# Two SwiGLU layers of a hybrid decoder: sums, norm rows and weight sums at other places, and the SP and GpSimd queues in the order of the program

## The chip, the cores and the metric

The kernel runs on one core of a Trainium2 chip. The metric is the device time of one execution in microseconds (us); the median of three runs of the kernel before is 1213.38 us, from 1211.77 to 1215.27.

## The reference

A decoder trunk of two layers over 512 tokens of width 1024, in float32:

```
h = h + recurrent_mixer(rms_norm(h, a_norm))
h = h + swiglu(rms_norm(h, a_ffn_norm), a_ffn_w_in, a_ffn_w_out)
k, v = shared_kv(h, ...)
h = h + dilated_attention_mixer(rms_norm(h, b_norm), ..., k, v, cos, sin)
h = h + swiglu(rms_norm(h, b_ffn_norm), b_ffn_w_in, b_ffn_w_out)

def swiglu(h, w_in, w_out):
    g, u = jnp.split(h @ w_in, 2, axis=-1)
    return (jax.nn.silu(g) * u) @ w_out
```

The hidden width of both SwiGLU layers is 2816, that is 22 blocks of 128. cos and sin are tables made from the token positions; only the attention reads them.

## The kernel before

**Precision.** Every float32 matrix is split into a high and a low part (`xh`, `xl` of the activations, `wh`, `wl` of a weight), and each product is three matmuls (`mm3`, L185 to L187). A weight of 512 KB goes HBM -> `wr` by DMA, `wr` -> `wh` by ScalarE (CAST, L133), and `wl = wr - wh` by VectorE (L140). There are two `wr` buffers and three of `wh` and `wl`.

**One SwiGLU layer** (`swiglu`, used twice; FFN1 and FFN2 below) is a list of steps. Four *plain* steps come first: blocks 0, 22, 1 and 23 of `h @ w_in`, with weights `plain 0` to `plain 3` (24 matmuls each). Then come five rounds of seven products in the manner of Strassen and Winograd, each for four hidden blocks: the weights of the products are GA, GB (gate halves), UB (an up half), and sums of them: S1 and S3 are loaded as a sum (one plain load from SP, then an accumulating DMA from GpSimd on top, L655 and L657), S2 = S1 + GA and S4 = GB + S2 are made in place by VectorE (L667). The activations' side of these sums are T1 to T4, made from `h`. A step "O" multiplies a finished chunk by `w_out` and subtracts it from `h`; a step "L" splits a chunk that has come back turned. Round 0 is `GA GB O S1 S2 O S3 S4 UB`, rounds 1 to 3 are `S1 GA GB L S2 O O S3 O S4 O UB`.

**What the norm needs.** The sum of squares `ssum` goes through four matmuls (L318) and nine small VectorE instructions (`norm_factors`); then eight VectorE instructions write two diagonal tiles (`dgh`, `dgl`), and two matmuls with ones spread the factors over the partitions into `rb` (`norm_rows`, L332 to L340). In FFN1 and FFN2 these two matmuls stand behind the third plain block. `rb` scales the plain blocks (`plain_pair`).

**What sets the order.** Inside `swiglu` TensorE, VectorE and ScalarE run in the order in which the program is written (`manual_schedule`). SP and GpSimd, which issue the DMAs, are not in that set: the scheduler of the compiler orders their queues. All plain loads go through SP's queue; an instruction there that waits for a buffer holds up those behind it. The big tiles GA, GB, S1, S3 and UB have one buffer each, in memory that the layer ahead of the SwiGLU gives back with its last `ssum` addition (L310). `Stream.load_to(i)` loads all pieces up to number i, counted from the first weight of the kernel; `swiglu` first sets how far loads (`al`, 4 pieces) and splits (`asp`, 2) run ahead.

**Tables.** `rotary` makes the cos and sin tables with some 30 small VectorE instructions at the first finished block of FFN1's last stage.

Of the kernel before, what the change touches and what calls it, by code (L numbers as in the profile page):

```python
# [20 lines left out]
ALU = mybir.AluOpType  # L21
# [36 lines left out]


class Held:  # L60


    def __init__(self, tc, engine):
        self.tc, self.engine, self.mark = tc, engine, None

    def __getattr__(self, op):
        fn, mark = getattr(self.engine, op), self.mark

        def run(*a, **k):
            inst = fn(*a, **k)  # L70
            behind(self.tc, inst, mark)
            return inst
        return run if mark is not None else fn
# [99 lines left out]
def trunk(tc, A, out):  # L173
    nc = tc.nc
    V, S, G, PE = Held(tc, nc.vector), Held(tc, nc.scalar), nc.gpsimd, nc.tensor

    def hold(mark, *fns):
        V.mark = S.mark = mark
        for fn in fns:
            fn()  # L180
        V.mark = S.mark = None
# [61 lines left out]
    with tc.tile_pool(name="keep", bufs=1) as kp, tc.tile_pool(name="wts", bufs=3) as wp, \  # L243
# [82 lines left out]
        def norm_rows(pool, r, tag="sq", bufs=1, copy=S.copy, hold=None, low=None, keep=None):  # L326
            dh, dl = (pool.tile([128, T], F32R, name=n, tag=g, bufs=b)
                      for n, g, b in (("dgh", tag, bufs), ("dgl", *(low or ("dgl", 1)))))
            ps = bank("O")
            for n in range(4):  # L330
                c = slice(128 * n, 128 * n + 128)
                V.tensor_scalar(dh[:, c], ident, r[:, n:n + 1], None, ALU.mult)  # L332
                a = V.scalar_tensor_tensor(dl[:, c], ident, r[:, n:n + 1], dh[:, c].bitcast(F32),
                                           ALU.mult, ALU.subtract)
            if hold:
                ws.hold[hold] = a
            PE.matmul(ps, ones_r, dh, start=True, stop=False)
            PE.matmul(ps, ones_r, dl, start=False, stop=True)
            rb = (keep or pool).tile([128, T], F32, name="rb", bufs=1)
            copy(rb, ps)  # L340
            return rb

# [14 lines left out]
        with tc.tile_pool(name="lru", bufs=2) as lp, \  # L357
# [66 lines left out]
            first.append(in_block(3, between=lambda: soon(norm_rows, lp, norm[0], "q", 3, V.tensor_copy, 4, ("q", 3))))  # L424
# [158 lines left out]
        def swiglu(fp, p, after):  # L583
# [75 lines left out]
            def split_weights(q, name, kk, hi, lo):  # L659
                n = name[:2]  # L660
                home = {"S2": "S1", "S4": "GB"}.get(n, n)

                def half(n):
                    return raws[q, n][:, :, 256 * kk:256 * kk + 256]

                def add(n, other):
                    V.tensor_tensor(half(n), half(n), half(other), ALU.add)  # L667

                if q == 0 and n in ("S2", "S4"):
                    add(*{"S2": ("S1", "GA"), "S4": ("GB", "S1")}[n])  # L670
                r = half(home).rearrange("q b (k c) -> q k b c", k=2)
                hi, lo = (x.rearrange("q (k b c) -> q k b c", k=2, b=4) for x in (hi, lo))
                S.copy(hi, r)  # L673
# [11 lines left out]
            def plain_block(j, b, i):  # L685
# [30 lines left out]
            def results(q, half, up, part):  # L716
# [5 lines left out]
                for i in range(2):  # L722
                    j = 2 * half + i
                    p.mark = V.transpose(turned[q][:, :, j], part[:, i].rearrange("q (b i) -> q b i", i=32))
# [18 lines left out]
            def product(q, name, first):  # L743
# [13 lines left out]
                if n in ("GA", "S2", "S3"):  # L757
                    part = acc["after " + n, q] = pair_tile()
                    for i in range(2):
                        S.copy(part[:, i], ps[i])  # L760
                        if n == "S3":
                            V.tensor_tensor(part[:, i], acc["S1", q][i], part[:, i], ALU.add)  # L762
# [9 lines left out]
            def out_block(c, m, i):  # L772
# [4 lines left out]
                for b in range(nb):  # L777
                    ps = bank("mm")
# [8 lines left out]
            for n in ("GA", "GB", "S1", "S3", "UB"):  # L787
                fetch(0, n)
            early = {0: make_t1, 1: make_t23, 2: low_t23, 3: lambda: plain_pair(0), 4: lambda: plain_pair(1),
                     6: lambda: (make_t4(), halve(d0, *homes["T4"]))}  # L790
            ordered = {mybir.EngineType.PE, mybir.EngineType.DVE, mybir.EngineType.Activation}
            with tc.manual_schedule(engines=ordered):
                for s, (kind, *what) in enumerate(p.steps):
                    {"plain": plain_block, "product": product, "out": out_block, "parts": parts_of}[kind](*what)
                    early.get(s, lambda: None)()

# [12 lines left out]
        with tc.tile_pool(name="tables", bufs=1) as rp:  # L809
            rp = Pool(rp)  # L810
            with tc.tile_pool(name="ffn1", bufs=2) as fp:
                fp = Pool(fp)
                tables = []

                def after_f1(m, ps):
# [3 lines left out]
                    if m == 0:  # L819
                        tables.extend(rotary(tc, A, rp, Temps(fp), p_f1.mark))  # L820

                swiglu(fp, p_f1, after_f1)
# [21 lines left out]
N_TMP = 5  # L844
# [7 lines left out]
def rotary(tc, A, rp, tp, mark):  # L852

    nc = tc.nc
# [4 lines left out]
    behind(tc, S.dma_start(far, A["far"]), mark)  # L859
    grow = rp.tile([128, 6, 128], F32, name="grow", bufs=1)  # L860
    behind(tc, S.dma_start(grow, A["row_gains"]), mark)
    V.tensor_scalar(grow[:, 3:6], grow[:, 3:6], -(128.0 ** -0.5), None, ALU.mult)


    pos = rp.tile([128, 8], I32, name="pos", bufs=1)
    behind(tc, S.dma_start(pos, A["pos"]), mark)
    inv = rp.tile([128, 16], F32, name="inv", bufs=1)
    behind(tc, S.dma_start(inv, A["inv_freq"]), mark)
    posf = rp.tile([128, 8], F32, name="posf", bufs=1)
    V.tensor_copy(posf, pos)  # L870
# [3 lines left out]
    tmp = [tp.tile([128, 512], F32, name="rtmp", tag="e", bufs=N_TMP) for _ in range(2)]  # L874
    ang, a1, a0, s1, k2, t = (tmp[i % 2][:, 128 * (i // 2):128 * (i // 2) + 128] for i in range(6))
# [15 lines left out]
    fma(s1, a0, -(2.0 ** 14), ang)  # L891
    rounded(a1, a0, 2.0 ** -9)
    fma(a0, a1, -512.0, a0)
    fma(s1, a0, m0[0], s1)
    fma(s1, a1, m1[0], s1)
    rounded(k2, s1, 1.0 / two_pi)
    fma(s1, k2, -c3[0], s1)
    fma(s1, a0, m0[1], s1)
    fma(s1, a1, m1[1], s1)
    fma(s1, k2, -c3[1], s1)  # L900
    rounded(t, s1, 1.0 / two_pi)
    fma(s1, t, -c3[0], s1)
    fma(s1, t, -c3[1], s1)
    V.tensor_add(k2, k2, t)
    fma(s1, a0, m0[2], s1)
    fma(s1, a1, m1[2], s1)
    fma(s1, k2, -c3[2], s1)
    V.scalar_tensor_tensor(t, s1, -1.0, s1, ALU.mult, ALU.max)
    V.tensor_scalar(t, t, -0.5, math.pi / 2.0, ALU.mult, ALU.add)
    S.activation(s1, s1, AF.Sin, scale=0.5)  # L910
    S.activation(t, t, AF.Sin)
    V.tensor_mul(a0, s1, t)
    V.tensor_mul(a1, s1, s1)
    for c in range(2):
        V.tensor_scalar(ss[:, :, c, :], a0.rearrange("q (c f) -> q c f", f=16), 4.0 * c - 2.0, None, ALU.mult)
# [446 lines left out]
```

## Time and profile before

| | |
|---|---|
| median of three runs | 1213.38 us |
| the profiled execution: its time | 1215.45 us |
| its span, first to last instruction | 1213.6 us |
| TensorE busy | 1171.2 us, 97% |
| VectorE busy | 854.5 us, 70% |
| ScalarE busy | 622.2 us, 51% |
| granted TensorE clock, mean | 0.987 |

The profiled execution took 1.85 us more than its span. The rows below name an engine, a line of the kernel and an operation, written as out<-in: `wl<-wr,wh` writes `wl`. PE is TensorE, DVE VectorE, ACT ScalarE, POOL GpSimd; SPq is the queue of DMA issues on SP. A timeline row begins with its start and its length in us; in brackets stands how long the engine was idle before and what ended that. "DMA to landing" is the time from the issue of a transfer to the arrival of its last byte.

### The profile page before, as it was taken

What the parts mean: (1) busy time and instruction counts of PE and PEld (TensorE: products, weight loads), DVE (VectorE), ACT (ScalarE), POOL (GpSimd) and SP (SyncE); (2) the same over time, 40 slices, a digit from 0 to 9 for tenths busy, and PEclk for the clock granted to TensorE, in tenths of its full rate; (3) what the DMA queues carried; (4) which work ended last, traced back from release to release, by engine and by line L of the source; (5) the groups of instructions that cost most, each with busy time, mean ns of one, the idle gap of its engine ahead of it and who ended that gap; (6) DMA issues with size and microseconds to landing.
All of it is one profiled execution on the core that took longest, in us unless ns stands there. A gap on an engine that the chain in (4) does not pass through costs nothing.

```text
span 1213.6 us, 15155 instructions
## 1 busy us (share of the span) xinstructions
PE 1171.2 (97%) x5403; PEld 961.5 (79%) x5403; DVE 854.5 (70%) x1525; ACT 622.2 (51%) x901; POOL 188.3 (16%) x221
## 2 busy tenths in 40 slices
PE   9999988899999999999999999999888999999998
PEld 6788876778888887788888887898767788888877
DVE  7987666686868686987565677765766867676764
ACT  6796444353535353575555677655443535353532
POOL 4210010110101000020411334341101101010000
PEclk9999999899999999999999999999898999999999
DMA  6643391857575732432988657435818575757224
GB/s 234 149 105 105 111 270 36 223 159 192 155 191 156 192 85 72 119 116 87 214 185 180 140 119 171 104 71 135 263 36 224 170 192 155 193 151 197 73 59 133
DMA packets 92235, 179.62 MB, mean 148 GB/s; under 512 B 8704, under 2 KB 27008, under 8 KB 92160
## 3 DMA queue, kind: packets, MB, share of 16 engines
q1 hardware_dynamic: 72144, 130.23, 33.3%
q0 software_dynamic: 18864, 47.19, 22.1%
q10 hardware_dynamic: 1152, 1.23, 0.4%
q8 instruction: 43, 0.70, 0.2%
q14 instruction: 32, 0.26, 0.1%
HBM read 164.99 MB, written 2.10 MB: 138 GB/s over the span
## 4 chain that ended last, share of the span: by engine, by line
PE 82%; DVE 9%; ACT 4%; DMA 3%; issue 2%; POOL 0%; DVEq 0%; ACTq 0%; POOLq 0%
PE ps L187 22%; PE ps L186 22%; PE ps L185 22%; PE ps L1025 5%; PE ps L1026 5%; PE ps L1027 5%; DMA S<-in_f_in 2%; DVE wl L674 1%; ACT wh L673 1%; PE ps L1104 1%; PE ps L1191 1%; DVE wl L140 1%; DVE xc L468 1%; ACT wh L133 1%; ACT pr L1177 0%
## 5 line engine op out<-in xcount | busy, mean ns | idle before, releaser
L133 ACT CAST wh<-wr 128x1024 fp32r<-128x1024 f32 (+2 forms) x136 | 131.0, 969 | 128.6 <-PE ps L186 77.9
L185 PE MATMUL ps<-wh,xh 128*128 128x512 f32 x320 | 126.8, 396 | 7.5 <-DVE e L762 7.5
L186 PE MATMUL ps<-wl,xh 128*128 128x512 f32 x320 | 126.4, 395 | 0.0
L187 PE MATMUL ps<-wh,xl 128*128 128x512 f32 x320 | 126.3, 395 | 0.0
L185 PE MATMUL ps<-gh,wh 128*128 128x512 f32 x288 | 113.9, 396 | 3.3 <-DVE h L785 3.3
L187 PE MATMUL ps<-gh,wl 128*128 128x512 f32 x288 | 114.6, 398 | 0.3
L186 PE MATMUL ps<-gl,wh 128*128 128x512 f32 x288 | 113.7, 395 | 0.0
L140 DVE TENSOR_TENSOR wl<-wr,wh 128x1024 fp32r<-128x1024 f32 (+2 forms) x93 | 99.9, 1084 | 15.8 <-ACT wh L133 15.4
L657 POOL DMA_DIRECT2D S<-in_f_in x40 | 48.4, 1290 | 386.8 <-DMA S<-in_f_in 167.9
L674 DVE TENSOR_TENSOR wl<-S,wh 128x1024 fp32r<-128x1024 f32 x60 | 73.3, 1225 | 47.2 <-ACT wh L673 47.2
L185 PE MATMUL ps<-xh,wh 128*128 128x512 f32 x256 | 103.5, 406 | 1.0 <-ACT xh L296 1.0
L673 ACT CAST wh<-S 128x1024 fp32r<-128x1024 f32 x60 | 62.8, 1050 | 79.3 <-PE ps L186 21.9
L185 PE MATMUL ps<-wh,T 128*128 128x512 f32 x240 | 95.6, 398 | 7.0 <-ACT wh L673 7.0
L186 PE MATMUL ps<-xl,wh 128*128 128x512 f32 x256 | 102.2, 399 | 0.1
L187 PE MATMUL ps<-xh,wl 128*128 128x512 f32 x256 | 101.9, 398 | 0.0
L186 PE MATMUL ps<-wl,T 128*128 128x512 f32 x240 | 95.8, 399 | 2.1 <-DVE wl L674 2.0
L187 PE MATMUL ps<-wh,T 128*128 128x512 f32 x240 | 95.0, 396 | 0.0
L1025 PE MATMUL ps<-wh,xh 128*128 128x512 f32 x224 | 91.5, 408 | 0.0
L1027 PE MATMUL ps<-wh,xl 128*128 128x512 f32 x224 | 87.8, 392 | 0.0
L1026 PE MATMUL ps<-wl,xh 128*128 128x512 f32 x224 | 87.4, 390 | 0.0
L673 ACT CAST wh<-GB 128x1024 fp32r<-128x1024 f32 x40 | 42.1, 1054 | 76.1 <-PE ps L187 50.9
L783 DVE TENSOR_TENSOR h<-h,ps 128x512 f32<-128x512 f32 x64 | 43.5, 685 | 51.4 <-PE ps L187 51.4
(284 smaller groups left out, 2702.9 us busy)
## 6 DMA issues: line engine op xcount, KB each, us to landing
S<-in_f_in SPq DMA_DIRECT2D x40, 512.0 KB, 4.7
S<-in_f_in POOLq DMA_DIRECT2D x40, 512.0 KB, 8.1
wr<-in_f_out SPq DMA_DIRECT2D x36, 512.0 KB, 4.4
wr<-in_w_q SPq DMA_DIRECT2D x28, 512.0 KB, 6.8
wl<-in_w_q POOLq DMA_DIRECT2D x28, 512.0 KB, 7.5
GA<-in_f_in SPq DMA_DIRECT2D x20, 512.0 KB, 4.6
GB<-in_f_in SPq DMA_DIRECT2D x20, 512.0 KB, 5.8
UB<-in_f_in SPq DMA_DIRECT2D x20, 512.0 KB, 5.2
```

The lines of the kernel that those rows point to most:

```text
L133: nc.scalar.copy(hi[:, c], r[:, c])
L140: a = eng.tensor_tensor(lo[:, c], r[:, c], hi[:, c].bitcast(F32), ALU.subtract)
L185: PE.matmul(ps, wh, xh, start=first, stop=False, skip_group_check=on)
L186: PE.matmul(ps, wh, xl, start=False, stop=False, skip_group_check=on)
L187: PE.matmul(ps, wl, xh, start=False, stop=last, skip_group_check=on)
L657: nc.gpsimd.dma_start(c, p.part(1, q, n == "S1", i), accum_op=ALU.add)
L673: S.copy(hi, r)
L674: V.tensor_tensor(lo, r, hi.bitcast(F32), ALU.subtract)
L783: V.tensor_tensor(by_time(x), by_time(x), in_turn(ps), ALU.subtract)
L1025: PE.matmul(ps[t], xh[k][:, r], wh[:, c], start=k == 0, stop=False)
L1026: PE.matmul(ps[t], xh[k][:, r], wl[:, c], start=False, stop=False)
L1027: PE.matmul(ps[t], xl[k][:, r], wh[:, c], start=False, stop=k == 7)
```

## The change

It touches both SwiGLU layers, and the tables only in FFN1.

- T1 is made ahead of the norm factors; the diagonal tiles are written right behind the factors, and the two spreading matmuls stand behind the second plain block instead of the third (with the copy of `rb` on ScalarE in both). `plain_pair(0)` and `(1)` run after the third and fourth step.
- In round 0 the in-place weight sums are made right behind the splits of S1 and S2, so one step earlier each, and T4 later.
- The fifth product's copy: what S3's addition needs of S1 is copied out right behind S1, and S3's own result is added from PSUM.
- One of the four blocks of round 0's "O" steps uses another PSUM bank; there are six temporaries instead of five.
- `rotary` becomes a generator whose pieces run between the steps of rounds 1 and 2 of FFN1.
- SP and GpSimd join the engines that keep the program's order, and the five fetches of round 0 stand at its head, with a `load_to(2)` and a `load_to(3)` between them.

```
-                if q == 0 and n in ("S2", "S4"):
-                    add(*{"S2": ("S1", "GA"), "S4": ("GB", "S1")}[n])
...
-                if q and n in ("GA", "GB"):
-                    add(*{"GA": ("S1", "GA"), "GB": ("GB", "S1")}[n])
+                second, fourth = ("GA", "GB") if q else ("S1", "S2")
+                if n == second:
+                    add("S1", "GA")
+                if n == fourth:
+                    add("GB", "S1")
                 if kk:
-                    gone = {"GA": "GA", "GB": "S1", "S4": "GB"} if q else {"S2": "GA", "S4": "S1 GB"}
-                    for x in {**gone, "S3": "S3", "UB": "UB"}.get(n, "").split():
+                    for x in {second: ["GA"], fourth: ["S1"], "S4": ["GB"], "S3": ["S3"], "UB": ["UB"]}.get(n, []):
                         fetch(q + 1, x)
...
                 if b == 0:
+                    make_t1()
                     p.r = norm_factors(fp)
-                elif b == 1:
-                    rows.append(norm_rows(temps, p.r, keep=fp))
+                    rows.extend(temps.tile([128, T], F32R, name=n) for n in ("dgh", "dgl"))
+                    diagonals(*rows, p.r)
+                elif b == HB:
+                    rows[:] = [spread(*rows, fp.tile([128, 768], F32, name="rb", bufs=1)[:, :T], S.copy)]
...
-                if n in ("GA", "S2", "S3"):
+                if n in ("GA", "S2", "S1"):
                     part = acc["after " + n, q] = pair_tile()
                     for i in range(2):
                         S.copy(part[:, i], ps[i])
-                        if n == "S3":
-                            V.tensor_tensor(part[:, i], acc["S1", q][i], part[:, i], ALU.add)
+                elif n == "S3":
+                    part = acc["after S3", q] = acc["after S1", q]
+                    for i in range(2):
+                        V.tensor_tensor(part[:, i], ps[i], part[:, i], ALU.add)
...
-                    ps = bank("mm")
+                    ps = bank("X" if b == 2 else "mm")
...
-            for n in ("GA", "GB", "S1", "S3", "UB"):
-                fetch(0, n)
-            early = {0: make_t1, 1: make_t23, 2: low_t23, 3: lambda: plain_pair(0), 4: lambda: plain_pair(1),
-                     6: lambda: (make_t4(), halve(d0, *homes["T4"]))}
-            ordered = {mybir.EngineType.PE, mybir.EngineType.DVE, mybir.EngineType.Activation}
-            with tc.manual_schedule(engines=ordered):
+            early = {1: make_t23, 2: lambda: (low_t23(), plain_pair(0)), 3: lambda: plain_pair(1),
+                     8: lambda: (make_t4(), halve(d0, *homes["T4"]))}
+            E = mybir.EngineType
+            with tc.manual_schedule(engines={E.PE, E.DVE, E.Activation, E.SP, E.Pool}):
+                ws.load_to(2)
+                fetch(0, "GA")
+                ws.load_to(3)
+                for n in ("GB", "S1", "S3", "UB"):
+                    fetch(0, n)
                 for s, (kind, *what) in enumerate(p.steps):
                     {"plain": plain_block, "product": product, "out": out_block, "parts": parts_of}[kind](*what)
                     early.get(s, lambda: None)()
+                    if s > 12:
+                        next(meanwhile, None)
...
-N_TMP = 5
+N_TMP = 6
```

By the time `swiglu` begins, more than 20 pieces have been loaded, so `load_to(2)` and `load_to(3)`, which count from the kernel's first weight, issue nothing.

**SP's queue at the start of FFN1.** First the order before, in which `wr26` and `wr27` are plain 2 and plain 3 and `wr32` is the first "O" weight:

```order
L116 DMA wr25_1328<-in_f1_in 128x1024
L116 DMA wr26_1401<-in_f1_in 128x1024
L116 DMA wr27_1403<-in_f1_in 128x1024
L109 DMA wr32_1592<-in_f1_out 128x4x256
L655 DMA GA_1379<-in_f1_in 128x2x512 x2
L655 DMA GB_1382<-in_f1_in 128x2x512 x2
L655 DMA S1_1385<-in_f1_in 128x2x512 x2
L655 DMA S3_1390<-in_f1_in 128x2x512 x2
L655 DMA UB_1395<-in_f1_in 128x2x512 x2
```

The same place in SP's queue of the changed kernel:

```order
L100 DMA wr25_1328<-in_f1_in 128x1024
L636 DMA GA_1381<-in_f1_in 128x2x512 x2
L636 DMA GB_1384<-in_f1_in 128x2x512 x2
L636 DMA S1_1387<-in_f1_in 128x2x512 x2
L636 DMA S3_1392<-in_f1_in 128x2x512 x2
L636 DMA UB_1397<-in_f1_in 128x2x512 x2
L100 DMA wr26_1401<-in_f1_in 128x1024
L100 DMA wr27_1403<-in_f1_in 128x1024
L93 DMA wr32_1600<-in_f1_out 128x4x256
```

Plain 2 and plain 3 moved from ahead of the ten fetches of round 0 to behind them.

**VectorE at the start of FFN1.** First a stretch of VectorE before, from the last addition to `ssum` (`wl26` is the split of plain 2, in front of it; `wt` and `T1` make T1; `nrv` begins the norm factors):

```order
L552 TENSOR_TENSOR h7_71<-h7_71,ps_1334 128x512
L140 TENSOR_TENSOR wl26_1410<-wr26_1401,wh26_1409 128x1024
L297 SCALAR_TENSOR_TENSOR xl_73<-h7_71,par_74,xh_72 128x512
L310 TENSOR_TENSOR ssum_78<-ssum_78,sq_1362 128x512
L320 TENSOR_SCALAR nrv_1442<-ps_1437 128x4
```

The same stretch of VectorE in the changed kernel, up to the first row of the norm factors:

```order
L533 TENSOR_TENSOR h7_71<-h7_71,ps_1334 128x512
L275 SCALAR_TENSOR_TENSOR xl_73<-h7_71,par_74,xh_72 128x512
L288 TENSOR_TENSOR ssum_78<-ssum_78,sq_1362 128x512
L124 TENSOR_TENSOR wl26_1410<-wr26_1401,wh26_1409 128x1024
L595 TENSOR_TENSOR wt_1376<-h0_64 128x256
L595 TENSOR_TENSOR wt_1376<-h1_65 128x256
L595 TENSOR_TENSOR wt_1376<-h2_66 128x256
L595 TENSOR_TENSOR wt_1376<-h3_67 128x256
L275 SCALAR_TENSOR_TENSOR T1_1373<-wt_1376,par_74,T1_1373 128x256 x4
L298 TENSOR_SCALAR nrv_1454<-ps_1449 128x4
```

The split of plain 2 moved behind the last `ssum`, and T1 ahead of the norm factors; behind these come the eight rows of the diagonal tiles.

**SP's queue in rounds 1 and 2 of FFN1.** `wr52`, `wr53`, `wr56` and `wr59` are round 1's four "O" weights, `wr70` and `wr71` round 2's first two. Before:

```order
L109 DMA wr52_2072<-in_f1_out 128x2x512
L655 DMA GA_1751<-in_f1_in 128x2x512 x2
L109 DMA wr53_2090<-in_f1_out 128x2x512
...
L655 DMA S1_2050<-in_f1_in 128x2x512 x2
L109 DMA wr56_2155<-in_f1_out 128x2x512
L109 DMA wr59_2242<-in_f1_out 128x2x512
L655 DMA S3_2193<-in_f1_in 128x2x512 x2
L109 DMA wr70_2515<-in_f1_out 128x2x512
L655 DMA GB_2269<-in_f1_in 128x2x512 x2
L109 DMA wr71_2533<-in_f1_out 128x2x512
```

In SP's queue of the changed kernel, where `S1_2066` is round 2's fetch of S1:

```order
L636 DMA S1_2066<-in_f1_in 128x2x512 x2
L93 DMA wr52_2088<-in_f1_out 128x2x512
L93 DMA wr53_2106<-in_f1_out 128x2x512
L93 DMA wr56_2180<-in_f1_out 128x2x512
L636 DMA S3_2220<-in_f1_in 128x2x512 x2
L93 DMA wr59_2272<-in_f1_out 128x2x512
L636 DMA GB_2298<-in_f1_in 128x2x512 x2
...
L636 DMA S1_2536<-in_f1_in 128x2x512 x2
L93 DMA wr70_2560<-in_f1_out 128x2x512
L93 DMA wr71_2578<-in_f1_out 128x2x512
```

In rounds 1 to 3 the first two "O" weights of a round moved from before the round's own products to behind the next round's S1 fetch, which waits until S2's second half has been split. Round 4 fetches nothing. FFN2 has the same orders.

More of the change, by code (lines that the diff above doesn't have):

```diff
@@ L324, in norm_factors, with diagonals @@
             return mean_squares(pool, [ssum[:, 128 * n:128 * n + 128] for n in range(4)], "nr")[1]
[L326 to L329, printed above, removed]
+        def diagonals(dh, dl, r):
             for n in range(4):
@@ L423, in trunk @@
             first.append(in_block(2, between=lambda: soon(norm_factors, small), at=6))
[L424 removed]
+            first.append(in_block(3, between=lambda: soon(norm_rows, lp, norm[0], 4)))
             rb = norm[1]
@@ L813, in trunk, with make_tables @@
                 tables = []
+                def make_tables():
+                    tables.extend((yield from rotary(nc, A, rp, fp)))
                 def after_f1(m, ps):
```

71 lines of the change are left out of this document (37 added, 34 removed).

## The prediction

> **What bounds the kernel now.** I read the first page of the profile, then the waits of TensorE, then its busy time in short windows, and last the queues that feed it. From the page, the busy times of the engines and the group of ScalarE's casts (busy and mean ns of one, behind the count):
>
> ```profile
> PE 1171.2 (97%) x5403; PEld 961.5 (79%) x5403; DVE 854.5 (70%) x1525; ACT 622.2 (51%) x901; POOL 188.3 (16%) x221
> ...
> L133 ACT CAST wh<-wr 128x1024 fp32r<-128x1024 f32 (+2 forms) x136 | 131.0, 969 | 128.6 <-PE ps L186 77.9
> ```
>
> TensorE is busy for 97% of the span, so the change, which removes no matmul, can win little: at most TensorE's idle time and the time at a low clock. TensorE's waits over the whole span (us in total, times, longest) say where that lies:
>
> ```profile
> PE ps L337 <- DVE dgh L332: 7.9, 2, 4.0
> PE ps L185 <- DVE e L762: 7.5, 4, 3.0
> PE ps L185 <- ACT wh L673: 7.0, 3, 2.9
> PE ps L185 <- DVE h L785: 3.3, 2, 1.7
> ...
> PE ps L186 <- DVE T L741: 1.1, 1, 1.1
> ```
>
> The first four are the change's targets. Counts of two to four say: once or twice per FFN, most of it in the first stage (plain steps and round 0). The windows of FFN1's round 0 show how much that is; I take FFN2 as alike. They give the stretch, its us, busy us of PE, PEld, DVE, ACT, POOL, then the granted clock, the DMA share and GB/s; the last row is a quiet round:
>
> ```profile
> 190.00:215.00 25.00, 19.98 (x74) 15.21 (x73) 18.41 (x24) 10.24 (x14) 0.00 (x0) 0.87 0.17 55
> 215.00:235.00 20.00, 16.97 (x68) 13.40 (x68) 12.08 (x13) 7.18 (x9) 2.41 (x2) 0.93 0.71 191
> 235.00:255.00 20.00, 18.01 (x77) 14.30 (x76) 14.09 (x17) 7.44 (x8) 4.64 (x6) 0.98 0.69 185
> 316.00:377.00 61.00, 60.97 (x267) 49.69 (x266) 43.22 (x49) 26.38 (x32) 7.11 (x8) 1.00 0.64 173
> ```
>
> Round 0 is idle for 5.02 + 3.03 + 1.99 = 10.0 us. The clock takes (1 - 0.87) x 25 + 0.07 x 20 + 0.02 x 20 = 5.05 us more. Rounds like the last row leave nothing to win: 60.97 of 61 us at clock 1.00. There a delay is all loss.
>
> **Part 1: the first stage.** SP's queue before, at the start of FFN1 (start, length of the issue):
>
> ```profile
> 155.12 0.39 SPq L109 DMA_DIRECT2D wr<-in_f_out  x1
> 156.44 0.89 SPq L655 DMA_DIRECT2D GA<-in_f_in  x2
> 157.37 0.98 SPq L655 DMA_DIRECT2D GB<-in_f_in  x2
> 158.39 3.05 SPq L655 DMA_DIRECT2D S<-in_f_in  x4
> 161.81 2.41 SPq L655 DMA_DIRECT2D UB<-in_f_in  x2
> 165.34 0.37 SPq L109 DMA_DIRECT2D wr<-in_f_out  x1
> ```
>
> Landings, from three views of one issue line in a short window: a plain load alone at 149.7; UB's two halves at 161.8 and 163.1; the weight behind them at 165.34.
>
> ```profile
> DMA to landing us min/median/max: 3.4/3.4/3.4
> DMA to landing us min/median/max: 11.0/11.8/12.5
> DMA to landing us min/median/max: 17.0/17.0/17.0
> ```
>
> UB's halves land at 161.81 + 11.0 = 172.8 and 163.1 + 12.5 = 175.6, so 2.8 us apart; the next weight lands at 165.34 + 17.0 = 182.3, another 6.7 us on. What is issued behind the fetches lands behind them, in order. In the changed kernel plain 2 stands in just that place. I take 177.0 for its landing: UB's second half, less some 1.4 us because the `in_f_out` weight of 155.12 is no longer ahead (two transfers of that size elsewhere land 1.3 us apart, part 2), plus 2.8 us for plain 2 itself. The ends of this last term are 1.3 us and 6.7 us.
>
> The Trainium skill ("DMA: Bandwidth & Descriptors", Queues, rings and completion order) says that a DMA engine takes turns between queues by packets. By that rule wide rows get more per turn, and plain 2 with rows of 1024 floats would pass the accumulating loads faster than UB with its 512: an estimated 1.4 us in place of 2.8, 2.8 us less in the sum for both layers. The trace agrees as far as two transfers go (2.8 us for 512-wide rows, 6.7 for 256).
>
> VectorE waits at the split of plain 2 for this landing, and behind it are queued T1, the norm factors and the diagonals, and behind these TensorE's spreading matmuls. The durations, from VectorE's timeline before:
>
> ```profile
> 159.19 0.16 DVE L320 TENSOR_SCALAR nrv<-ps 128x4 f32<-128x4 f32 x1 [2.84 <-PE ps L318]
> ...
> 160.86 1.42 DVE L614 TENSOR_TENSOR wt<-h 128x256 f32<-128x256 f32 x4
> 162.20 1.67 DVE L297 SCALAR_TENSOR_TENSOR T<-wt,par,T 128x256 fp32r<-128x256 f32 x4
> 164.08 1.23 DVE L140 TENSOR_TENSOR wl<-wr,wh 128x1024 fp32r<-128x1024 f32 x1 [0.21 <-ACT wh L133]
> ...
> 171.68 0.28 DVE L332 TENSOR_SCALAR dgh<-ident,nry 128x128 fp32r<-128x128 f32 x1
> ```
>
> And from TensorE's, the end of the third plain block and the spreading matmul:
>
> ```profile
> 169.81 0.39 PE L187 MATMUL ps<-xh,wl 128*128 128x512 f32 x1
> 174.11 0.59 PE L337 MATMUL ps<-dgh,ones_r 128*128 128x512 f32 x1 [3.92 <-DVE dgh L332]
> ```
>
> Cast 1.0, split 1.2, T1 162.20 + 1.67 - 160.86 = 3.0, factors 160.86 - 159.19 = 1.7, diagonals 174.11 - 171.68 = 2.4: 9.3 us. So the spreading starts at 177.0 + 9.3 = 186.3 instead of 174.11: +12.2. In front of it now stand two plain blocks, behind it two instead of one, and a block (24 matmuls) takes 5.5 us (61 us for 267 is 0.228 each): +5.5. Together 17.7 us.
>
> Against that stand the 10.0 + 5.05 = 15.1 us of round 0. With plain 2 this late, everything that round 0 waited for has come in the meantime: the fetches have landed, the sums are made a step earlier. I count all of it as gone (if S2 still waited, 2.9 us of it would stay). What is late next is GB's first split. Between the diagonals and it VectorE has, by order, four splits and two sums of T2 and T3 of the same size (6 x 1.23), two groups as long as T1's second (2 x 1.67), and both pairs:
>
> ```profile
> 187.50 0.68 DVE L703 SCALAR_TENSOR_TENSOR w<-ps,rb 128x512 f32<-128x512 f32 x1
> 188.49 0.69 DVE L704 TENSOR_TENSOR w<-w,g 128x512 f32<-128x512 f32 x1 [0.30 <-ACT g L702]
> 190.29 1.23 DVE L302 TENSOR_TENSOR gl<-w,gh 128x1024 fp32r<-128x1024 f32 x1 [1.11 <-ACT gh L301]
> ```
>
> That is 7.4 + 3.3 + 2 x (0.68 + 0.68 + 0.69) + 1.23 + waits of 2 x 0.30 + 1.11 = 17.8 us, against 2 x 0.59 + 3 x 5.5 = 17.7 us until TensorE wants it. So nothing if nothing else comes between; ScalarE, which makes T2, T3, two silus and the casts in the same stretch, can add some us. I take 2 us, with ends of 0 and 4.5. Net per FFN: 17.7 - 15.1 + 2 = +4.6, for both **+9.2** (ends: +2.6 with 1.3 us and 0; +22 with 6.7 us and 4.5).
>
> **Part 2: the "O" weights of rounds 1 to 3.** In the changed kernel the first two stand behind the next S1 fetch, and that waits for the split of S2's second half. Before, in round 1 of FFN1, first that fetch, then the matmul that first uses the weight:
>
> ```profile
> 324.08 0.88 SPq L655 DMA_DIRECT2D S<-in_f_in  x2
> ```
>
> ```profile
> 329.70 0.40 PE L185 MATMUL ps<-gh,wh 128*128 128x512 f32 x1
> ```
>
> Landings of the fetch's halves, and of an `in_f_out` weight issued at 330.33 beside accumulating loads:
>
> ```profile
> DMA to landing us min/median/max: 3.6/4.1/4.5
> DMA to landing us min/median/max: 6.2/6.2/6.2
> ```
>
> The halves land at 324.08 + 3.6 = 327.7 and 324.5 + 4.5 = 329.0, 1.3 us apart. The weight is issued at 324.08 + 0.88 = 324.96 and lands 1.3 us behind them, at 330.3. Cast 1.0: 331.3, and TensorE wanted it at 329.70. Split 1.2: 332.5, and TensorE's third matmul (0.23 each) wanted it at 330.2. So 2.3 to 2.5 us are lost, six times: **+15**. Ends: 0.6 if it lands 3.6 us after its issue, 3.2 if 6.2. Nothing covers it: the row of the quiet round has 0.03 us of idle time.
>
> The clock may add to that. Two windows of FFN1, one around the 2.9 us wait of S2 and one with 2 us of idle time:
>
> ```profile
> 208.00:212.00 4.00, 2.92 (x6) 2.03 (x7) 2.36 (x2) 1.50 (x2) 0.00 (x0) 0.56 0.02 4
> 244.00:248.00 4.00, 2.01 (x8) 1.15 (x7) 2.03 (x2) 2.94 (x3) 0.00 (x0) 1.00 0.45 175
> ```
>
> Behind 2.9 us the clock was 0.56, with 2 us it stayed at 1.00. The 2.5 us here come in two pieces (1.6 at the cast, 0.8 at the split), each shorter than 2, so I count no loss; the other end is 1.5 us each. The Trainium skill ("TensorE: Matmul & The Clock Gate", What's actually happening) puts the drop to half clock behind an idle window of about 3.4 us. By that rule too nothing would be lost here; the 2.9 us that cooled the clock are shorter than it says, so the measurement decides.
>
> **Part 3: the rest.** The fourth sum is asked for one step earlier: the wait for `e` (L762) was 7.5 us in four, 3.0 twice in round 0 (counted above), the rest 1.5: -1.5. The tables leave FFN1's end, where T waits: -1.1. In rounds 1 and 2 their pieces cost nothing, since VectorE is busy 43.2 of 61 us there (an end of +2, if a piece stands ahead of an urgent split). The fifth product's copy, the bank and the sixth temporary: nothing; an addition from PSUM takes the place of a copy and an addition in SBUF. Together **-2.6**.
>
> **The sum**: +9.2 + 15 - 2.6 = +21.6 us. The profiled execution took 1215.45 us, so 1237 of its own; the median of the runs is 1213.38, so 1235 there.
>
> **The rivals.**
>
> *Forecast (0.62):* as above, 1235 us.
>
> *Loads overtake (0.09), faster.* If a load issued behind the fetches lands as quickly as one alone, plain 2 is issued at 164.2 (161.81 + 2.41) and lands at 167.6 instead of 177.0: 9.4 us less per FFN, and the "O" weights land 3.4 us after issue, at 328.4, in time for the cast. Then 2 x (4.6 - 9.4) - 2.6 = -12.2: 1201 us. It decides from a landing before 173.7 (2 x 1.3 = 2.6) with the weights in time, before 170.8 with them late. The weight of 165.34 with its 17.0 us speaks against it; for it, only that this weight has narrow rows.
>
> *Only the first stage pays (0.14).* If the weights land before the halves of S1 or TensorE is late anyway, part 2 is nothing: 1213.4 + 9.2 - 2.6 = 1220 us. For it: 3.6 us of landing is near enough that 0.6 would be left.
>
> *Slower still (0.15).* The pauses of part 2 cool the clock (6 x 1.5 = 9) and plain 2 takes 6.7 us (2 x 3.9 = 7.8): 1252 us.
>
> That the change doesn't do what it says holds for two lines: `load_to(2)` and `load_to(3)` issue nothing, and the sum has that in it.
>
> **How the numbers follow.** The likeliest gives 1235. The ends of all terms together would be 1217 and 1262; 1218 to 1254 leaves out the rival on the other side and about one in ten of the rest. A change of 0.3%, 3.6 us, is what a measurement can tell here (the runs spread from 1211.77 to 1215.27). Faster: 0.09, the loads that overtake. Same: 0.04, the low end of the third case. Slower: 0.87.
>
> **What would show it.** In the changed kernel, at the start of FFN1: a split of plain 2 that waits on VectorE until about 179; one wait of TensorE for `dgh` of some 20 us per FFN; no wait at S2 or S4 in round 0, and a short one at GB. In rounds 1 to 3, waits of 1.6 and 0.8 us at the first "O" of a round, three times per FFN, at clock 1.00. The forecast is wrong if plain 2 lands before 174, if the first "O" of a round doesn't wait, or if round 0 keeps its waits behind the long one (then up to 30 us more).

## The result, and the profile after

The changed kernel takes 1245.77 us (median of 4 runs, 1243.57 to 1249.07), the kernel before 1214.29 us beside it; the ratio is 1.0265, with a 95% interval of 1.0234 to 1.0296. So it is slower by 31.5 us, where +21.6 was forecast. The profiled execution, the fastest of the four, has a span of 1241.0 us, 27.4 more than before.

From the page of the changed kernel, the busy times, and TensorE's waits over the whole span (us in total, times, longest):

```profile
PE 1167.8 (94%) x5403; PEld 960.5 (77%) x5403; DVE 852.6 (69%) x1525; ACT 624.4 (50%) x901; POOL 189.3 (15%) x221
```

```profile
PE ps L314 <- DVE dgh L307: 43.8, 2, 21.9
PE ps L163 <- ACT wh L117: 14.5, 6, 2.8
PE ps L164 <- DVE wl L653: 1.9, 2, 0.9
```

The four waits of before (for `dgh`, `e`, S2's `wh`, `h`) have become two: one of 21.9 us per layer, for the diagonals, and six of some 2.4 us for the cast of an "O" weight. The third, 0.9 us, is GB's split, the next late thing.

**The long wait.** In the changed kernel, UB's two loads and the two plain ones behind them in SP's queue at FFN1's start, and the landings of UB's (issued from 158.52) and of plain 2 (issued at 161.64):

```profile
158.52 1.53 SPq L636 DMA_DIRECT2D UB<-in_f_in  x2
161.64 1.67 SPq L100 DMA_DIRECT2D wr<-in_f_in  x2
```

```profile
DMA to landing us min/median/max: 11.2/12.3/13.4
DMA to landing us min/median/max: 13.8/13.8/13.8
```

Plain 2 lands at 161.64 + 13.8 = 175.4, 2.6 us behind UB's second half (159.4 + 13.4 = 172.8). From there on ScalarE, VectorE and TensorE, each from its own timeline:

```profile
175.83 1.04 ACT L117 CAST wh<-wr 128x1024 fp32r<-128x1024 f32 x1 [22.43 <-DMA wr<-in_f_in]
```

```profile
176.90 1.23 DVE L124 TENSOR_TENSOR wl<-wr,wh 128x1024 fp32r<-128x1024 f32 x1 [22.64 <-ACT wh L117]
178.04 1.43 DVE L595 TENSOR_TENSOR wt<-h 128x256 f32<-128x256 f32 x4
```

```profile
185.14 0.77 PE L314 MATMUL ps<-dgh,ones_r 128*128 128x512 f32 x1 [21.92 <-DVE dgh L307]
```

It is the chain that the prediction worked out, link by link: landing, cast, split, and 7.1 us of T1, norm factors and diagonals behind the split (178.04 to 185.14). VectorE stood idle for 22.6 us ahead of it.

**The six waits.** Round 1 of FFN1: SP's fetch of S1 and the weights behind it; the first weight's landing; the cast; the first matmuls:

```profile
265.43 0.88 SPq L636 DMA_DIRECT2D S<-in_f_in  x2
266.35 8.91 SPq L93 DMA_DIRECT2D wr<-in_f_out  x3
```

```profile
DMA to landing us min/median/max: 6.1/6.1/6.1
```

```profile
272.57 1.04 ACT L117 CAST wh<-wr 128x1024 fp32r<-128x1024 f32 x1 [3.13 <-DMA wr<-in_f_out]
```

```profile
273.67 0.49 PE L163 MATMUL ps<-gh,wh 128*128 128x512 f32 x1 [2.77 <-ACT wh L117]
274.33 0.76 PE L164 MATMUL ps<-gl,wh 128*128 128x512 f32 x1 [0.17 <-issue]
274.93 0.80 PE L165 MATMUL ps<-gh,wl 128*128 128x512 f32 x1
```

The wait is one piece of 2.77 us, and the matmuls behind it run 0.6 to 0.8 us each instead of 0.39. The windows say why (the stretch, its us, busy us of PE, PEld, DVE, ACT, POOL, the granted clock, the DMA share, GB/s; the first two rows are round 0, where there had been 10 us of idle time):

```profile
190.00:215.00 25.00, 24.06 (x106) 19.41 (x105) 17.98 (x21) 13.86 (x17) 0.00 (x0) 1.00 0.00 0
215.00:245.00 30.00, 30.00 (x133) 24.69 (x132) 26.28 (x35) 15.32 (x20) 4.79 (x4) 1.00 0.73 202
```

```profile
274.00:278.00 4.00, 3.83 (x10) 2.76 (x10) 3.89 (x6) 2.80 (x4) 0.00 (x0) 0.57 1.10 199
278.00:282.00 4.00, 4.00 (x19) 3.23 (x18) 1.14 (x3) 0.63 (x1) 0.00 (x0) 1.00 0.38 131
```

Behind the pause the clock is at 0.57 for 4 us. Round 0 is as good as free of waits.

Where the 27.4 us come from, by the start of the same matmul in both timelines:

| place | before | after | later by |
|---|---|---|---|
| kernel's start, 20 us in | 21.60 | 20.17 | -1.4 |
| FFN1, spreading | 174.11 | 185.14 | 11.0 |
| FFN1, round 1's S1 | 247.25 | 249.21 | 2.0 |
| behind the first O of round 1, 2, 3 | 280.13, 331.63, 392.42 | 286.78, 342.09, 406.99 | 6.7, 10.5, 14.6 |
| FFN1, last stage | 496.52 | 507.82 | 11.3 |
| attention | 738.89 | 749.78 | 10.9 |
| FFN2, round 1's S1 | 943.83 | 959.17 | 15.3 |
| behind the first O of round 1, 2, 3 | 967.91, 1028.23, 1090.42 | 987.74, 1052.20, 1118.93 | 19.8, 24.0, 28.5 |
| FFN2, last stage | 1160.12 | 1187.74 | 27.6 |

So the first stages cost 2.0 + 1.4 = 3.4 and 15.3 - 10.9 = 4.4 us, together +7.8. The six O steps cost 12.6 and 13.2 us, together +25.8. The rest is negative: about 3.3 us at the end of FFN1, 0.9 at the end of FFN2, and 2 us outside the change. The medians lie 4.1 us further apart than these two spans (31.5 against 27.4); no profile shows where.

### The profile page after: what moved, and what is told of

Its sections match the earlier page's. It is cut to its first block, busy times and chain, and to the rows that moved or that the text cites. A ratio compares the mean times of both kernels' runs of the same rounds, so it can differ in the third digit from the quotient of the medians.

```text
span 1241.0 us, 15125 instructions
## 1 busy us (share of the span) xinstructions
PE 1167.8 (94%) x5403; PEld 960.5 (77%) x5403; DVE 852.6 (69%) x1525; ACT 624.4 (50%) x901; POOL 189.3 (15%) x221
## 3 DMA queue, kind: packets, MB, share of 16 engines
q0 software_dynamic: 18864, 47.19, 21.6%
## 4 chain that ended last, share of the span: by engine, by line
PE 78%; DVE 8%; DMA 7%; ACT 4%; issue 2%; SPq 1%; POOL 0%; ACTq 0%; DVEq 0%
PE ps L164 21%; PE ps L165 21%; PE ps L163 20%; PE ps L1031 5%; PE ps L1032 5%; PE ps L1033 5%; DMA wr<-in_f_out 3%; DMA wr<-in_f_in 2%; DVE wl L653 1%; DMA GB<-in_f_in 1%; ACT wh L117 1%; ACT wh L652 1%; PE ps L1110 1%; PE ps L1197 1%; DVE xc L449 1%
## 5 line engine op out<-in xcount | busy, mean ns | idle before, releaser
L163 PE MATMUL ps<-gh,wh 128*128 128x512 f32 x288 | 117.3, 407 | 14.5 <-ACT wh L117 14.5
L164 PE MATMUL ps<-gl,wh 128*128 128x512 f32 x288 | 118.1, 410 | 0.8 <-issue 0.5
L165 PE MATMUL ps<-gh,wl 128*128 128x512 f32 x288 | 118.0, 410 | 0.1
L652 ACT CAST wh<-S 128x1024 fp32r<-128x1024 f32 x60 | 63.0, 1050 | 75.6 <-PE ps L164 30.3
L653 DVE TENSOR_TENSOR wl<-S,wh 128x1024 fp32r<-128x1024 f32 x60 | 73.1, 1222 | 32.7 <-ACT wh L652 32.7
L165 PE MATMUL ps<-wh,T 128*128 128x512 f32 x240 | 93.5, 390 | 0.0
L163 PE MATMUL ps<-wh,T 128*128 128x512 f32 x240 | 93.5, 390 | 0.0
L163 PEld LDWEIGHTS ps<-gh,wh 128*128 128x128 f32 x288 | 56.2, 195 | 29.6 <-ACT wh L117 17.1
```

What stands on the lines that cost most here:

```text
L163: PE.matmul(ps, wh, xh, start=first, stop=False, skip_group_check=on)
L164: PE.matmul(ps, wh, xl, start=False, stop=False, skip_group_check=on)
L165: PE.matmul(ps, wl, xh, start=False, stop=last, skip_group_check=on)
```

## Experiments

**The two places in SP's queue.** If the order of SP's queue is the whole cost, two small edits must remove it. The first puts plain 2 and plain 3 where their two lines stand, by counting from the layer's first weight:

```
-                ws.load_to(2)
+                ws.load_to(p.steps[0][3] + 2)
                 fetch(0, "GA")
-                ws.load_to(3)
+                ws.load_to(p.steps[0][3] + 3)
```

> The changed kernel with plain 2's and plain 3's loads where their two lines stand, ahead of the fetches (both layers). Theory A (plain 2's late landing makes the 21.9 us wait for the diagonals, and the sums made earlier have really removed round 0's waits): the wait falls to about 2 us, 20 us less per layer, and round 0 stays free of waits: 1245.8 - 42 = about 1204 us. Rival B (the long stall only hid round 0's waits, everything else being as late as before): up to 15 us per layer come back, 1234 us.

Measured: 1203.19 us, ratio to the kernel before 0.989 (0.9864 to 0.9916). TensorE's waits:

```profile
PE ps L163 <- ACT wh L117: 14.8, 6, 3.0
PE ps L163 <- ACT wh L652: 2.2, 2, 1.1
PE ps L164 <- DVE wl L653: 1.9, 2, 0.9
```

The wait for the diagonals is gone and round 0's old waits do not come back; only GB is waited for (L652, L653). Theory A, to within a microsecond. The stall was not what had hidden round 0's waits.

The second moves the S1 fetch of rounds 1 to 3 from GB's second split to S2's (in round 0 `fourth` is S2 already):

```
-                    for x in {second: ["GA"], fourth: ["S1"], "S4": ["GB"], "S3": ["S3"], "UB": ["UB"]}.get(n, []):
+                    for x in {second: ["GA"], "S2": ["S1"], "S4": ["GB"], "S3": ["S3"], "UB": ["UB"]}.get(n, []):
```

> The changed kernel with the next round's S1 fetch written at S2's second split in rounds 1 to 3, so that the first two O weights stand ahead of it in SP's queue. Theory A: the six waits for the cast (14.5 us) go, and the half clock behind them (about 1.9 us each) too: 1245.8 - 25.8 = 1220 us; the wait at the start of each layer stays 21.9. Rival B (S1 now comes two transfers later and its round waits for it): part of the gain is seen as waits at S1 or S2 of the next round, 1230 us or more. Rival C (bandwidth, not order, makes the weights late): 1245 us.

Measured: 1220.89 us, ratio 1.0046 (1.0027 to 1.0064). The waits, and the window behind the first O of round 1:

```profile
PE ps L314 <- DVE dgh L307: 43.2, 2, 21.8
PE ps L165 <- DVE wl L124: 2.1, 3, 1.4
```

```profile
274.00:278.00 4.00, 4.00 (x19) 3.23 (x18) 2.73 (x6) 0.00 (x0) 1.13 (x1) 1.00 0.98 203
```

All six waits for the cast are gone, the clock stays at 1.00 and the next round's S1 doesn't wait: theory A. The S1 fetch could not start any earlier at the old place, since it waits for S2's second split anyway; it only held up the two weights behind it.

Both edits together:

> Both edits of the last two kernels. Theory A: the effects add, 1245.8 - 42 - 25.8 = about 1178 us, faster than the kernel before by some 36 us. Rival B (round 0's waits come back): 1208 us.

Measured: 1176.08 us, ratio 0.9666 (0.9638 to 0.9694). What is left of TensorE's waits is short: the two at GB, as with the first edit, and, longest of all, one for a split in an O step:

```profile
PE ps L165 <- DVE wl L124: 2.5, 3, 1.6
```

The two effects add. So the change holds a gain of some 39 us on the kernel before, and two orders in SP's queue turned it into a loss of 31. The control is the reverse edit, the changed kernel with SP and GpSimd left to the compiler's scheduler:

```
-            with tc.manual_schedule(engines={E.PE, E.DVE, E.Activation, E.SP, E.Pool}):
+            with tc.manual_schedule(engines={E.PE, E.DVE, E.Activation}):
```

> The changed kernel with SP and GpSimd out of the engines that keep the program's order, all else as changed. Theory A (only the order of SP's queue costs): plain 2 and the O weights are loaded early again, about 1178 to 1185 us. Rival B (the moved sums, norm rows and tables cost time by themselves, or only hide behind the stall): 1208 us or more.

Measured: 1178.21 us, ratio 0.9683 (0.9657 to 0.971), not to be told from the kernel with both edits. Keeping SP in program order is worth nothing in itself; written in the wrong order it costs 70 us.

**Inside the two waits.** Nine extra matmuls in front of each of the six O steps, whose result is overwritten, fill the pause and leave the weight as late as it is:

```
                 for b in range(nb):
                     ps = bank("X" if b == 2 else "mm")
+                    if b == 0 and c in (1, 2, 3) and m == 0:
+                        for _ in range(9):
+                            PE.matmul(ps, sums[0][:, 0, 0:128], sums[0][:, 1], start=True, stop=True)
```

> The changed kernel with nine extra matmuls (their result is overwritten) ahead of the first O of rounds 1 to 3, 2.05 us of work inside pauses of 2.1 to 2.8 us. The weight arrives as late as before; only the clock is kept up. Theory A (the half clock behind each pause is a cost of its own, 1.75 us, but hides the wait for the split, 0.8 us, which would show at full clock): 6 x 1.0 less, 1245.8 - 6 = about 1240 us, with short waits for the split appearing. Rival B (the clock is the whole of it): 1235 us. Rival C (the split would be waited for just as long, the clock costs nothing): 1246 us. If the pauses were not idle time of TensorE at all, the nine matmuls would add up to 12 us: 1258.

Measured: 1238.16 us, ratio 1.0173 (1.0148 to 1.0197): 7.6 us less than the changed kernel by the medians, 5.3 by the spans, 11 by the ratios, so the time alone does not tell A from B. The window behind the pause, the waits, and the first matmuls of the O step in round 1:

```profile
274.00:278.00 4.00, 2.75 (x11) 1.83 (x11) 2.95 (x5) 3.78 (x5) 0.00 (x0) 1.00 1.07 174
```

```profile
PE ps L163 <- ACT wh L117: 2.8, 5, 1.0
```

```profile
271.80 2.20 PE L767 MATMUL ps<-T 128*128 128x512 f32 x9
274.96 0.49 PE L163 MATMUL ps<-gh,wh 128*128 128x512 f32 x1 [0.96 <-ACT wh L117]
275.63 0.47 PE L164 MATMUL ps<-gl,wh 128*128 128x512 f32 x1 [0.17 <-issue]
276.23 0.50 PE L165 MATMUL ps<-gh,wl 128*128 128x512 f32 x1
```

The waits fall from 14.5 to 2.8 us, since matmuls fill them, and the clock stays at 1.00. By the start of the same matmul in both timelines, an O step wins 0.9 to 1.5 us, and the six together 6.7: near theory A's 6, and not the 10.5 of the clock alone. At full clock the first matmul with `wl` starts 1.27 us behind the first with `wh` (276.23 against 274.96), where two matmuls of 0.23 would make 0.46, so the split is waited for by 0.8 us. In the changed kernel the same two matmuls lie 1.26 us apart (273.67 and 274.93): there the half clock of the first matmuls falls inside the wait for the split. An O step's 4.3 us are 2.4 of pause, 0.8 for the split and 1.1 of clock.

For the long wait, splits run one piece ahead at a layer's start, so that plain 2's split stands behind the diagonals on VectorE:

```
-            ws.asp, ws.al = 2, 4
+            ws.asp, ws.al = 1, 4
...
                 if b == 0:
+                    ws.asp = 2
                     make_t1()
```

> The changed kernel with splits running one piece ahead instead of two at the start of each layer, so that T1, the norm factors and the diagonals stand ahead of plain 2's split on VectorE; SP's queue stays as changed. Theory A (the wait of 21.9 us is plain 2's landing plus the 8.2 us queued behind its split): the spreading comes at once, and TensorE waits for the cast or split of plain 2 instead, until about 176 to 178, some 9 us earlier than 185.1: 1245.8 - 2 x 9 = about 1228 us. Rival B (something else than the landing holds VectorE): the wait stays near 22 us, 1245 us.

Measured: 1232.88 us, ratio 1.0129 (1.0104 to 1.0154): 12.9 us less than the changed kernel by the medians. TensorE's first wait in FFN1:

```profile
177.37 0.80 PE L163 MATMUL ps<-xh,wh 128*128 128x512 f32 x1 [12.74 <-ACT wh L117]
```

The wait for the diagonals is gone. Plain 2's cast is waited for instead, 12.7 us, and plain 2 starts 8.8 us earlier than in the changed kernel. So of the 21.9 us, 13 are the landing with the cast, and 9 the split and what was queued behind it. Of the 18 us expected 13 were seen: the lead of 8.8 us has shrunk to 6.9 by the end of plain 2, of which 13 matmuls run at half clock (7 in the changed kernel), and to 6.2 by GB's first cast, which is waited for by 0.5 us.

**What the gain of 39 us is made of.** From the kernel with both edits, one part of the change at a time was taken back. First the weight sums of round 0, back at the splits of S2 and S4, and with them GA's and S1's fetches for round 1:

```
+                if not q and n in ("S2", "S4"):
+                    add(*{"S2": ("S1", "GA"), "S4": ("GB", "S1")}[n])
...
-                second, fourth = ("GA", "GB") if q else ("S1", "S2")
+                second, fourth = ("GA", "GB") if q else ("", "")
...
+                    gone = {"GA": ["GA"], "S2": ["S1"], "S4": ["GB"]} if q else {"S2": ["GA"], "S4": ["S1", "GB"]}
```

> The fastest kernel so far (both mended places, 1176.1 us) with the weight sums of round 0 back at the splits of S2 and S4. By the waits of the kernel before: S2's cast 2.9 and split 0.5 and the half clock behind them, about 3 us, per layer: 1176.1 + 12 = 1188 us. If the sums are hidden anyway once the loads come early: 1176.

Measured: 1206.49 us, ratio 0.9915 (0.9885 to 0.9945): 30 us, more than twice what the old waits gave. TensorE at round 1's S1, and SP's fetch of it:

```profile
240.73 0.80 PE L163 MATMUL ps<-wh,T 128*128 128x512 f32 x1 [9.53 <-ACT wh L654]
```

```profile
220.48 0.95 SPq L636 DMA_DIRECT2D S<-in_f_in  x2
```

With the sums late, S1's buffer comes free at S4's split instead of S2's; its fetch goes out at 220.48, behind S3's, where it went out at 202.91 with both edits. Round 1 waits 9.5 us for it, and S2 isn't waited for at all. The sums' worth is the early fetch, not the wait of S2. The kernel before had the sums late too, but TensorE came to round 1's S1 only at 244.8 there, not at 231.2, and waited 1.2 us.

The fifth product's copy:

```
-                if n in ("GA", "S2", "S1"):
+                if n in ("GA", "S2", "S3"):
...
+                        if n == "S3":
+                            V.tensor_tensor(part[:, i], acc["S1", q][i], part[:, i], ALU.add)
```

> The fastest kernel so far with the fifth product's copy back behind S3. The prediction held this edit for nothing and put the waits for e (7.5 us in four) down to the sums: then 1176 us. Rival: the fourth sum's product goes on in S1's PSUM banks, which VectorE still reads behind S3, so the waits for e are this edit's: 7.5 us and the half clock behind the two long ones, 2 x 1.9: 1176.1 + 11 = 1187 us.

Measured: 1183.11 us, ratio 0.9724 (0.9697 to 0.975): 7 us. The waits for `e` are back, so they belong to this edit, if shorter than in the kernel before:

```profile
PE ps L163 <- DVE e L746: 3.6, 4, 1.4
```

They make up half of the 7 us; where the other half lies isn't shown.

Norm rows, T1 and plain pairs (`early` as before, diagonals and spreading behind the third block):

```
                 if b == 0:
-                    make_t1()
                     p.r = norm_factors(fp)
+                elif b == 1:
...
-                elif b == HB:
```

> The kernel with both places mended (1176.1 us) with T1, the diagonals, the two spreading matmuls and the plain pairs back at the steps where the kernel before had them. By the prediction's rows: the wait for the diagonals, 3.9 us, and the half clock behind it, about 1.7 us, and the backlog that they leave for round 0 come back in each layer: 1176.1 + 11 = 1187 us or a little more. If the rest of the change had made that wait harmless: 1176 us.

Measured: 1185.27 us, ratio 0.9763 (0.9744 to 0.9782): 9 us, near what the rows gave:

```profile
PE ps L314 <- DVE dgh L307: 9.4, 2, 4.8
```

The waits at GB (some 2 us per layer) are gone in exchange, so the wait for the diagonals by itself costs more than the 9 us.

The bank:

```
-                    ps = bank("X" if b == 2 else "mm")
+                    ps = bank("mm")
```

> The kernel with both places mended, with the third block of round 0's O steps in the bank that it had before. By the wait for h in the kernel before (3.3 us in two): 1176.1 + 3.3 = 1179.4 us. If that wait was due to the late VectorE and not to the bank: 1176 us.

Measured: 1198.96 us, ratio 0.9863 (0.9842 to 0.9884): 23 us, where 3.3 were expected. The waits, and VectorE around the first of them:

```profile
PE ps L163 <- DVE h L771: 11.3, 4, 3.2
```

```profile
188.88 1.23 DVE L653 TENSOR_TENSOR wl<-S,wh 128x1024 fp32r<-128x1024 f32 x1 [2.89 <-ACT wh L652]
190.14 1.22 DVE L648 TENSOR_TENSOR S<-S,GA 128x1024 f32<-128x1024 f32 x1
...
194.31 1.23 DVE L653 TENSOR_TENSOR wl<-S,wh 128x1024 fp32r<-128x1024 f32 x1 [1.74 <-ACT wh L652]
195.57 1.23 DVE L648 TENSOR_TENSOR S<-S,GA 128x1024 f32<-128x1024 f32 x1
196.71 1.88 DVE L771 TENSOR_TENSOR h<-h,ps 128x512 f32<-128x512 f32 x3
```

With the sums at their new place, VectorE reads an O block's bank (L771) only behind two splits and two sums. With the three banks of `mm` TensorE stands still at the fourth block in each of round 0's O steps, 2.7 to 3.2 us and half clock behind it; with a fourth bank it goes on. So the bank and the moved sums seem to belong together: it pays more because VectorE reads late. No run took both back.

The tables:

```
-                swiglu(fp, p_f1, after_f1, make_tables())
+                swiglu(fp, p_f1, after_f1)
...
+                    if m == 0:
+                        for _ in made:
+                            pass
```

> The kernel with both places mended, with all pieces of the tables made at the first finished block of FFN1's last stage again. By the wait for T in the kernel before: +1.1 us at FFN1's end; against it the wait of 1.6 us for a split in round 1, which a piece of the tables would have caused, goes: 1175.6 us, within the error of 1176. If the tables were hidden in rounds 1 and 2 and cost more than that wait at the end: 1178 us.

Measured: 1176.62 us, ratio 0.9682 (0.9665 to 0.9699), not to be told from the kernel with both edits. But this run does not have the tables where the kernel before had them. There VectorE made most of them from 481.9 to 491.8, ahead of T, and TensorE waited for T and then for `h`:

```profile
490.84 0.94 DVE L885 SCALAR_TENSOR_TENSOR rtmp<-rtmp 128x128 f32<-128x128 f32 x3
492.08 2.50 DVE L741 TENSOR_TENSOR T<-T,T 128x512 fp32r<-128x512 f32 x4 [0.30 <-ACT wh L133]
```

```profile
492.82 0.50 PE L186 MATMUL ps<-T,wh 128*128 128x512 f32 x1 [1.08 <-DVE T L741]
496.52 0.47 PE L185 MATMUL ps<-T,wh 128*128 128x512 f32 x1 [0.89 <-DVE h L783]
```

In this run the program has the tables at FFN1's first finished block, but VectorE ran them from 163.0 to 222.5, in the plain steps and round 0. The first piece stands among the diagonals and waits there for its own transfer, and the spreading is late by 2.4 us, though its row names another releaser:

```profile
162.99 0.36 DVE L873 TENSOR_SCALAR grow<-grow 128x384 f32<-128x384 f32 x1 [2.68 <-DMA grow<-in_row_gains]
```

```profile
165.31 0.47 PE L314 MATMUL ps<-dgh,ones_r 128*128 128x512 f32 x1 [2.21 <-DMA GB<-in_f_in]
```

Against that, the wait of 1.6 us for a split in round 1, ahead of which a piece of the tables stood, is gone (1.9 us by the start of the same matmul). The two about cancel, by chance. So the tables cost some 2 us at each of these two places; what they cost at the place that they had before is read from its trace alone.

Last, the wait at GB. T2's and T3's low parts stood on VectorE ahead of the plain pairs, and so ahead of GB's splits:

```
-            early = {1: make_t23, 2: lambda: (low_t23(), plain_pair(0)), 3: lambda: plain_pair(1),
+            early = {1: make_t23, 2: lambda: plain_pair(0), 3: lambda: plain_pair(1), 4: low_t23,
```

> The kernel with both places mended, with the low parts of T2 and T3 (2.4 us on VectorE) made behind GA's step instead of ahead of the first plain pair, so that GB's splits stand ahead of them. It meets the wait that the prediction named as the next late one, GB's first cast and split (1.1 and 0.9 us, with half clock behind it some 1.9 more, in each layer): 1176.1 - 7 = 1169 us. If VectorE then lacks the time ahead of S1, so that the O step or S1 wait: 1174 us or more.

Measured: 1173.31 us, ratio 0.9658 (0.9642 to 0.9674). It is 2.8 us less than the kernel with both edits, where 7 were expected. No wait at GB is left among TensorE's; the longest for a split is in an O step:

```profile
PE ps L165 <- DVE wl L124: 1.9, 2, 1.5
```

By the timelines the two layers win 3.8 and 2.3 us at GB, and FFN1's first O step gives 0.7 back. The expected half clock behind the two waits was there in FFN1 alone: in the kernel with both edits the clock over the 4 us from the second wait on (182 to 186, 861 to 865) was 0.57 in FFN1 and 1.00 in FFN2. The intervals of this kernel and the one with both edits overlap (0.9642 to 0.9674 and 0.9638 to 0.9694), so the times alone don't show it. It is the fastest median of all, 41 us under the kernel before.

## Why the prediction came out as it did

- **Direction and mechanism, part 1: right.** The landing was forecast at 177.0 and came at 175.4, the spreading at 186.3 and came at 185.14, the wait at GB at 2 us and was 0.9. The net was forecast as +9.2 and is +7.8. (Its low end should read +2.2, not +2.6, by the prediction's own terms.) Without plain 2's place in the queue the stall is not there (first experiment), and its two halves, the landing with the cast and the split with its queue, were taken apart (sixth experiment). That round 0's waits go was right, but one reason given, that all else had come in the meantime, isn't needed: they stay away without the stall as well. The other, the sums made a step earlier, holds (taken back, they cost 30 us). What the Trainium skill ("DMA: Bandwidth & Descriptors", Queues, rings and completion order) was taken to give, 1.4 us for plain 2 behind UB, the trace does not bear out: 2.6 us, close to the 2.8 between UB's halves in the kernel before.
- **Part 2: right in place, wrong in size.** Forecast +15, measured +25.8. The step that failed is "I count no loss" of clock. It rested on the pause coming in two pieces, each shorter than 2 us, and on a row with 2 us of idle time at clock 1.00, which held two waits, of 1.22 and 0.77 us. The first piece, 1.6 us by the forecast, came as 2.1 to 2.8 us, as the weight landed 7.0 us behind the start of the fetch ahead of it (266.35 + 6.1 - 265.43) and not 6.2, and such a pause cools the clock: 0.57 for 4 us. With the later landing and the clock the sum is what was measured: 2.4 + 0.8 + 1.1 = 4.3 us each (the forecast's other end for the clock was 1.5). The rival that priced the clock, 1252 us, was wrong in its other half: plain 2 did not take 6.7 us.
- **Part 3: about the right sum for the wrong reasons.** Forecast -2.6, measured some -4. The waits for `e` were put down to the sums and the fifth product's copy was held for nothing; taking the copy back brings them back (7 us in all). The bank was held for nothing too; taken back in the kernel with both edits, it costs 23 us. The sixth temporary was taken back by no run. The tables were given 1.1 us, the wait for T. By the traces, FFN1's end of the kernel before had three waits that the changed kernel hasn't: 0.7 us for `e`, 1.1 for T and 0.9 for `h`; between the same matmuls they come to the 3.3 us won there. The tables ran just ahead of the last two, so their place looks to be worth some 2.6 us, but no run has put them back there. What they cost in rounds 1 and 2, where the prediction gave an end of +2, shows in the kernel with both edits: one wait of 1.6 us for a split.
- **The rivals.** Loads that overtake: no, UB and plain 2 landed in the order of issue. (Its bound of 170.8 with late weights leaves out the first stage's +9.2; by the prediction's terms it is 166.2, below the 167.6 that this rival gave.) Only the first stage pays: no, the six O steps cost 25.8 us.
- **What the prediction didn't see:** with round 0 cleared of waits, the early sums and the further bank are worth 30 and 23 us, not the 12 and 3.3 us that the rows of before gave. For the sums the traces show that a slower round 0 had covered this.

## What to carry to other kernels

A queue put into program order takes over whatever order the program happens to have: read that order, and for each load name the wait of the instruction in front of it and the engine that will miss it. A price read from the old trace's waits holds only as long as the rest is as slow as it was; parts of a change taken back one by one (30 + 23 + 9 + 7 us of a gain of 39) need not add up. A pause of TensorE like the six here (2.1 to 2.8 us) costs its length and a stretch of low clock behind it, less the waits that the low clock then hides. And look in the trace where a moved piece really runs: the tables that were put back in the program ran on VectorE some 300 us ahead of that place.

## What the runs showed of the hardware

The shortest of the six pauses, in round 2 of FFN1 of the changed kernel, and the window around it:

```profile
338.53 0.50 PE L163 MATMUL ps<-gh,wh 128*128 128x512 f32 x1 [2.06 <-ACT wh L117]
```

```profile
336.00:345.00 9.00, 6.81 (x22) 4.71 (x21) 4.45 (x5) 4.01 (x5) 1.53 (x2) 0.81 1.01 249
```

2.06 us without a matmul were enough for the clock to drop, to a mean of 0.81 over 9 us. The Trainium skill ("TensorE: Matmul & The Clock Gate", What's actually happening) speaks of an idle window of about 3.4 us; the pauses here are shorter, so the measurement decides. Nine matmuls whose result nobody uses kept the clock at 1.00.

Shorter pauses went both ways. At the third matmul of round 1's first O step TensorE waited 1.55 us in the run with the norm rows back, and 1.57 us in the kernel with both edits. The windows behind these two pauses:

```profile
256.00:260.00 4.00, 4.00 (x11) 3.18 (x12) 3.05 (x5) 0.26 (x1) 1.61 (x2) 0.57 0.78 154
```

```profile
252.00:256.00 4.00, 3.85 (x17) 3.12 (x18) 3.83 (x7) 0.27 (x1) 1.79 (x2) 1.00 0.63 123
```

The clock halved behind the first and stayed full behind the second, so the length of a pause alone doesn't tell what it costs.
